# A hybrid decoder layer on one core: each attention pair projects its keys before its values, and the values of the last pair move into steps 44 to 48

## The chip, the cores and the metric

The kernel runs on one core of one Trainium2 chip. TensorE (PE) multiplies matrices, VectorE (DVE) and ScalarE (ACT) work on whole tiles and read the matmul results out of the PSUM banks, GpSimd (POOL) helps with plain elementwise work, and SyncE (SP) issues all the DMAs, in order, from one queue. Every engine works through its own list of instructions in the order in which the program wrote them, and waits on semaphores where an operand comes from another engine.

The metric is the time of one execution on the device in microseconds. Before the change it is 1214.67 us, the median of three runs (1214.23 to 1215.04).

## The reference

One decoder layer for 1024 tokens of width 1024, in fp32. The input is normalised and multiplied by one wide matrix; its columns feed two mixers, whose outputs are joined, normalised (the attention half), multiplied by the output matrix, normalised and added to the input. A squared-ReLU MLP of width 4096 follows in the same way.

```python
h = rmsnorm(x, mix_pre_norm)
q_a, k_a, v_a, q_h, f_h, i_h, g_h = split(h @ w_in)
attn = rmsnorm(dilated_mixture_attention(q_a, k_a, v_a, slopes), attn_out_norm)
rec  = hgrn2_recurrence(q_h, f_h, i_h, g_h, lower_bounds, hgrn_out_norm)
x = x + rmsnorm(concat([attn, rec]) @ w_out, mix_post_norm)
x = x + rmsnorm(square(relu(rmsnorm(x, mlp_pre_norm) @ w_ff1)) @ w_ff2, mlp_post_norm)
```

The attention has 8 heads of 64 columns. Each head mixes three causal windows, (window, dilation) = (128, 1), (512, 4) and (2048, 16), weighted by their softmax denominators. The recurrence has 4 heads of 128 columns with a gated state.

## The kernel before

**Precision.** The matmuls work on pairs of fp32r tiles: a value is split into a high part (ACT copies it) and a low part (DVE or POOL subtracts the high part from the value), and a product is three matmuls, high by high, low by high and high by low (`three_pass`, lines 89 to 91). So each weight block must be split before use: `w_split` copies on ACT (line 85) and subtracts on DVE (line 86), and then issues the load of a later raw block (line 106). `w_get(i, ahead)` splits all blocks of the weight stream up to number i + ahead. The blocks 16 to 27 are the query, value and key columns of the four pairs of heads; 28 to 35 are the eight row blocks of the output matrix (`WO0` is 28).

**Stages.** First come the four recurrence heads, then 64 attention steps, then the second part of the output product, the norms, and the MLP. The attention works in pairs of heads. For each pair, `attn_proj` (line 728) is a Python generator that emits the projections: queries, the values of the first 512 tokens, both halves of the keys, and the values of the other 512 tokens. One call emits one unit, which is three matmuls of 512 columns, and a 512-token half of a projection has eight units. After the eighth unit the PSUM bank is read: `keys_read` for the keys, line 747 for the queries (followed by two ACT copies and two POOL subtractions), line 764 for the values.

**The filler queue.** The generators stand in a list, `queue`, and `fill` (line 172) takes units from it. A generator that yields None stops the filling for that call. So the units are put between the attention work, step by step, as PE's filler: `UNITS` (line 1236) gives the number for each of the 64 steps, one half of them in the middle of the step and the others at its end. Two conditions stop the queue: the queries of pair 2 and 3 wait for `second_done`, the keys of a pair wait for `first_done` of the pair ahead, which is set in step 3 of its 16 steps, when those keys' slabs come free.

**The steps.** Each head has eight steps, one for each item: four blocks of local attention (D0 to D3), two far parts (F0, F1) and two near parts (N0, N1). A step takes the exponentials of the next item (`raise_`, ACT, line 892), multiplies queries by keys for a later item (`look`, PE; its maximum is taken on DVE, line 842), transposes the item's weights (`turn`, PE; copies on ACT and subtractions on DVE), multiplies the item before by the values (`weigh`), and finishes an earlier one (`finish`). The maximum of a far row is joined with that of the near rows between the items 0 and 4: `spread_max` (DVE, line 865) in items 0 and 2, `swap_max` (PE) in items 1 and 3, `joint` (DVE, lines 878 and 879) in items 3 and 4. The exponentials of the far part need `joint`. A PSUM bank with a look's result comes free when DVE has taken the maximum. At most one key job (half a pair's key split: ACT, POOL and two DMAs) runs per step.

**The values.** `values_turn` (line 712) transposes a half's values on PE, copies them on ACT (line 719) and subtracts on DVE (line 720). The transposed values of a pair are stored to DRAM (`v_dram`, line 723) and read back in another order by `far_load` (line 642), for the far parts. The first use is the product of F0, in step 5 of the pair's first head. `far_load` runs after the last turn for pair 0, in steps 15 and 31 for the pairs 1 and 2, and in the hook of step 48 for pair 3.

**Hooks.** `hooks` (line 1214) is an order written out by hand: what else a step does. Steps 0 and 2 multiply the gate of the last recurrence head. Steps 43 to 54 prepare the early output product: the recurrence half of the first 512 rows is loaded (`early_rows`, line 1007), scaled on POOL (`row_rec`), transposed and split (`row_turn`), and multiplied by the first four row blocks of the output matrix (`early_out`, 32 units), which then serve as filler up to step 63. `early_rows` and `early_sums` use buffers of the input's transposed blocks (`hT`), and so can only stand where the projections of the first token half, or of both, are done.

## Time and profile before

| what | us |
|---|---|
| median of three runs | 1214.67 |
| the profiled execution | 1214.51 |
| its span | 1212.7 |
| PE busy in the span | 1198.3 |
| DVE busy | 868.8 |
| ACT busy | 546.6 |
| POOL busy | 326.3 |

The recurrence ends and the attention steps start at about 306 us of the span; the steps end at about 520 us. The granted PE clock is full throughout. In a row of the timeline stand start, duration, engine, line, operation, output and inputs, shapes and count; a bracket at its end gives the idle time of the engine before it, and what ended it. In a row of the table by stretches stand the stretch, its length, the busy time of PE, of PE's weight loads, of DVE, ACT and POOL with their instruction counts, the PE clock, the DMA share and GB/s.

### The profile page before, as it was taken

Reading aid. Unit: us, or ns where it says so; the run is one execution under the profiler, and the core shown is the slowest. Engines: PE = TensorE matmul, PEld = TensorE weight load, DVE = VectorE, ACT = ScalarE, POOL = GpSimd, SP = SyncE. Lnnn points to the kernel's source line nnn. Section 1 sums busy time; section 2 is a strip of 40 time slices with the busy share of each in tenths; the row PEclk is TensorE's granted clock in tenths of the full one; section 3 lists DMA queues with packets and bytes.
Section 4 is the critical chain, followed back from the end, with each engine's and each line's share of the span. In section 5 each row is a group of like instructions: output and inputs, shape, how many; then the busy total and the mean of one; then the engine's idle time right before and its main releaser. Section 6 shows DMA issues by size and latency. Waiting matters only on the chain.

```text
span 1212.7 us, 17220 instructions
## 1 busy us (share of the span) xinstructions
PE 1198.3 (99%) x6350; PEld 1026.8 (85%) x6350; DVE 868.8 (72%) x1478; ACT 546.6 (45%) x1067; POOL 326.3 (27%) x321
## 2 busy tenths in 40 slices
PE   8999999999999999999999999999999999999998
PEld 8898989888888887888888888888888888888886
DVE  5697878777666767677689566766678554478796
ACT  7633333322565657755565222222234453534562
POOL 0110102022221213254230886575631000000022
PEclk9999999999999999999999999999999999999999
DMA  5231323123544546364514555553587534433337
GB/s 218 69 94 58 104 75 108 36 82 75 141 109 117 141 118 146 104 218 145 188 64 156 182 174 209 192 185 140 199 324 266 212 92 152 158 102 100 109 104 278
DMA packets 86483, 174.21 MB, mean 144 GB/s; under 512 B 12160, under 2 KB 38784, under 8 KB 86400
## 3 DMA queue, kind: packets, MB, share of 16 engines
q1 hardware_dynamic: 86400, 173.12, 44.0%
q8 instruction: 50, 0.82, 0.3%
q14 instruction: 33, 0.27, 0.1%
HBM read 117.76 MB, written 49.04 MB: 138 GB/s over the span
## 4 chain that ended last, share of the span: by engine, by line
PE 93%; DVE 2%; ACT 2%; DMA 1%; issue 1%; POOL 0%; SPq 0%; DVEq 0%; POOLq 0%; ACTq 0%
PE f L1940 18%; PE f2s L1940 7%; PE pig L91 2%; PE pig L89 2%; PE pig L90 2%; PE pl L480 2%; PE pwo L91 2%; PE pwo L89 2%; PE pwo L90 2%; PE pm_ak L89 1%; PE pm_f L89 1%; PE pm_ak L91 1%; PE pm_ak L90 1%; PE pm_f L91 1%; PE pm_f L90 1%; PE pm_av L89 1%
## 5 line engine op out<-in xcount | busy, mean ns | idle before, releaser
L86 DVE TENSOR_TENSOR al<-ar,ah 128x1024 fp32r<-128x1024 f32 x56 | 70.6, 1261 | 80.7 <-ACT ah L85 80.6
L1940 PE MATMUL f<-bh,ah 128*128 128x512 f32 x320 | 124.5, 389 | 0.0
L1940 PE MATMUL f<-bl,ah 128*128 128x512 f32 x320 | 124.5, 389 | 0.0
L1940 PE MATMUL f<-bh,al 128*128 128x512 f32 x320 | 124.5, 389 | 0.0
L85 ACT ACTIVATE ah<-ar 128x1024 fp32r<-128x1024 f32 x56 | 59.1, 1056 | 87.5 <-DMA ar<-actd 87.2
L1940 PEld LDWEIGHTS f<-bh,al 128*128 128x128 f32 x320 | 60.1, 188 | 12.6
L1940 PEld LDWEIGHTS f<-bl,ah 128*128 128x128 f32 x320 | 60.1, 188 | 12.5
L1940 PEld LDWEIGHTS f<-bh,ah 128*128 128x128 f32 x320 | 60.1, 188 | 12.3
L2014 POOL TENSOR_SCALAR lbl<-ssq 128x1 f32<-128x1 f32 x4 | 3.3, 819 | 245.7 <-ACT fd L2010 245.6
L1563 POOL TENSOR_TENSOR e<-x,e 128x512 f32<-128x512 f32 x14 | 21.6, 1540 | 131.0 <-DVE x L1514 123.8
L1940 PE MATMUL f2s<-bl,ah 128*128 128x512 f32 (+1 forms) x128 | 48.9, 382 | 0.0
L1940 PE MATMUL f2s<-bh,al 128*128 128x512 f32 (+1 forms) x128 | 48.9, 382 | 0.0
L1940 PE MATMUL f2s<-bh,ah 128*128 128x512 f32 (+1 forms) x128 | 48.9, 382 | 0.0
L671 POOL COPY tout<-traw 128x256 f32<-128x256 f32 x16 | 12.2, 763 | 107.9 <-DMA traw<-in_bias_tab_dram 74.2
L991 POOL TENSOR_TENSOR anat<-anat,stat 128x128 f32<-128x128 f32 (+1 forms) x24 | 13.4, 559 | 102.4 <-DVE anat L990 91.1
L86 DVE TENSOR_TENSOR bl<-br,bh 128x1024 fp32r<-128x1024 f32 x32 | 40.1, 1253 | 1.1 <-ACT bh L85 1.0
L1957 ACT ACTIVATE acc<-f 128x512 f32<-128x512 f32 x28 | 16.7, 598 | 49.4 <-PE f L1940 49.4
L86 DVE TENSOR_TENSOR wl<-raw,wh 128x1024 fp32r<-128x1024 f32 x23 | 30.1, 1310 | 10.9 <-ACT wh L85 10.9
L85 ACT ACTIVATE bh<-br 128x1024 fp32r<-128x1024 f32 x32 | 33.6, 1050 | 3.7 <-PE f L1940 2.4
L707 POOL TENSOR_TENSOR kl<-kf,kh 64x512 fp32r<-64x512 f32 x16 | 22.2, 1390 | 39.8 <-ACT kh L706 36.8
L751 POOL TENSOR_TENSOR ql<-qf,q 64x512 fp32r<-64x512 f32 x16 | 21.4, 1340 | 42.4 <-ACT q L750 41.8
L89 PE MATMUL pwo<-woh,mt 128*128 128x512 f32 x80 | 31.6, 395 | 0.0
(1702 smaller groups left out, 4022.5 us busy)
## 6 DMA issues: line engine op xcount, KB each, us to landing
ar<-actd SPq DMA_DIRECT2D x56, 512.0 KB, 3.7
br<-in_w_ff_dram SPq DMA_DIRECT2D x16, 1024.0 KB, 6.3
w1r<-in_w_ff_dram SPq DMA_DIRECT2D x14, 1024.0 KB, 6.5
raw<-in_w_in_dram SPq DMA_DIRECT2D x26, 512.0 KB, 4.0
actd<-e SPq DMA_DIRECT2D x17, 768.0 KB, 4.3
actd<-e SPq DMA_DIRECT2D x11, 1024.0 KB, 4.1
vd<-v SPq DMA_DIRECT2D x16, 256.0 KB, 3.9
raw<-in_w_out_dram SPq DMA_DIRECT2D x8, 512.0 KB, 3.7
```

Of the source, the lines that this page charges most:

```text
L85: S.activation(hi, src, AF.Copy)
L86: eng.tensor_tensor(out=lo, in0=src, in1=f32(hi), op=ALU.subtract)
L89: TE.matmul(dst, lhs[0], rhs[0], start=start, stop=False)
L90: TE.matmul(dst, lhs[0], rhs[1], start=False, stop=False)
L91: TE.matmul(dst, lhs[1], rhs[0], start=False, stop=stop)
L480: TE.matmul(pl[:, n % 2, :192], kt[:, n * P:(n + 1) * P], sets[u // 2][:, n % 4], start=True, stop=True)
L707: G.tensor_tensor(out=kl[a:b], in0=src, in1=f32(kh[a:b]), op=ALU.subtract)
L751: G.tensor_tensor(out=lo[a:b], in0=full[a:b], in1=f32(stacks[i]["q"][a:b, sl]), op=ALU.subtract)
L991: G.tensor_tensor(out=dst, in0=dst, in1=st["rd"][:, b].unsqueeze(2).to_broadcast([P, n, 64]), op=ALU.mult)
L1563: eng[0].tensor_tensor(out=e1[:, 3], in0=a21, in1=e1[:, 2], op=ALU.add)
L1940: TE.matmul(pm, a[:, j, c], b[:, j, d], start=start and j == 0 and q == 0, stop=stop and j == 1 and q == 2, skip_group_check=True)
L1957: S.activation(acc_at(p, i), pm, AF.Copy)
```

## The change

The change reorders the work of the attention stage; the matmuls, their operands and their number stay.

- The weight stream has the key columns ahead of the value columns in each pair, and `attn_proj` projects queries, both halves of the keys, then both halves of the values. All the keys of a pair, and with them all its values, now stand behind the condition on `first_done`.
- A half of the values is transposed during the second half's projection, the other half during the queries of the next pair. Each half is stored on its own: four stores of four blocks, and four stores of two blocks (the last two blocks are not needed). `far_load` reads all of the first tile, then the second, and is called in steps 18 and 34 for the pairs 1 and 2.
- For the last pair the values run in steps 44 to 48; the last turn and `far_load` stand in the hook of step 49, and the early output products start there. `early_rows` is called when the first half of these values is done.
- Output block 0 and 1 get slabs of their own, block 2 and 3 the shared weight buffers; they are split in the hooks of steps 42, 46, 48 and 50, the third with its subtraction on POOL. Before, it was 44, 45, 47 and 48.
- The last gate is multiplied in four pieces, in steps 0 to 3. A key job may run in all items but 0 and 5. `UNITS` has other numbers.

```diff
@@ the weight stream
-    for i in range(4 * HH, 4 * HH + 3 * (AH // 2)):
-        stream.append((w_in[i], None))
+    for i in range(4 * HH, 4 * HH + 3 * (AH // 2), 3):
+        for n in (0, 2, 1):
+            stream.append((w_in[i + n], None))
     WO0 = len(stream)
-    WO_TAG = (None, ("S", "S"), ("S", "BT"), None, ("S", "S"), ("S", "T"), ("T", "T"), ("T", "T"))
+    WO_TAG = (("S", "S"), ("S", "BT"), None, None, ("S", "S"), ("S", "T"), ("T", "T"), ("T", "T"))
@@ hgrn_core: gated(g4) in halves becomes gated(g2) in quarters
...
@@ far_load
-        for odd in range(2):
-            for c, p0, k0, n in ((0, 0, 64 * odd, P), (1, 0, P - P * odd, 64), (1, 64, P - P * odd, 64)):
...
+        for c in range(2):
+            for odd in range(2):
+                for c_, p0, k0, n in ((0, 0, 64 * odd, P), (1, 0, P - P * odd, 64), (1, 64, P - P * odd, 64)):
+                    if c_ == c:
...
@@ values_turn
-        if hf == 1:
-            for r in range(DIL):
-                nc.sync.dma_start(out=v_dram[pr][r].rearrange("(n i) c -> i n c", i=32),
-                                  in_=f32(vs[32 * r:32 * r + 32]).rearrange("p n h a d -> p n (h a d)"))
-            if pr == 0:
-                far_load(0)
+        b = slice(0, 4) if hf == 0 else slice(4, 6)
+        for r in range(DIL):
+            nc.sync.dma_start(out=v_dram[pr][r].rearrange("(n i) c -> i n c", i=32)[:, b],
+                              in_=f32(vs[32 * r:32 * r + 32, b]).rearrange("p n h a d -> p n (h a d)"))
+        turned_v[pr] += 1
+        if pr == 0 and hf == 1:
+            far_load(0)
@@ attn_proj, behind the queries
+        while pr > 0 and not first_done[pr - 1]:
+            yield None
+        wk = w_get(A0 + 3 * pr + 1, 0)
...
+        for hf in range(2):
+            for n, cost in enumerate(proj_t(wk, f"ak{pr}", hf, box)):
+                if n == 4 and hf == 0:
+                    w_get(A0 + 3 * pr + 1)
+                yield cost
+            keys_read(pr, box[0], hf)
+            yield 650.0
+        wv = w_get(A0 + 3 * pr + 2, 0)
+        for hf in range(2):
             for n, cost in enumerate(proj_t(wv, f"av{pr}", hf, box)):
-                if n == 4:
-                    w_get(A0 + 3 * pr + 1 + hf)
+                if n == 3 and hf == 1:
+                    values_turn()
+                    cost += 450.0
+                if n == 4 and hf == 0 and pr < AH // 2 - 1:
+                    w_get(A0 + 3 * pr + 2)
                 yield cost
...
-        yield from values(0)
-        while pr > 0 and not first_done[pr - 1]:
-            yield None
...
-        yield from values(1)
@@ hooks
         0: lambda: last_gate(0),
-        2: lambda: last_gate(1),
-        43: lambda: row_rec(0),
-        44: lambda: [row_rec(1), w_get(WO0, 0)],
-        45: lambda: w_get(WO0 + 1, 0),
-        46: lambda: row_turn(0, 0),
-        47: lambda: [drain(), w_get(WO0 + 2, 0), early_sums(), queue.extend(early_out(t) for t in range(NE))],
-        48: lambda: [values_turn("t"), far_load(AH // 2 - 1), w_get(WO0 + 3, 0), row_rec(2)],
-        49: lambda: [load_bias(AH - 1), row_rec(3)],
-        50: lambda: row_turn(1, 0),
-        52: lambda: [row_turn(2, 0), load_gain("gmix", "R", g_mix)],
-        54: lambda: row_turn(3, 0),
+        1: lambda: last_gate(1),
+        2: lambda: last_gate(2),
+        3: lambda: last_gate(3),
+        42: lambda: w_get(WO0, 0),
+        46: lambda: [w_get(WO0 + 1, 0), row_rec(0)],
+        47: lambda: [row_turn(0, 0), row_rec(1)],
+        48: lambda: [drain(), w_split(G)],
+        49: lambda: [values_turn("t"), far_load(AH // 2 - 1), early_sums(),
+                     queue.extend(early_out(t) for t in range(NE))],
+        50: lambda: [w_get(WO0 + 3, 0), row_rec(2), load_bias(AH - 1)],
+        51: lambda: row_rec(3),
+        52: lambda: [row_turn(1, 0), load_gain("gmix", "R", g_mix)],
+        54: lambda: row_turn(2, 0),
         55: lambda: [w_get(WO0 + 4, 0), row_load(0)],
-        57: lambda: [row_load(1), row_norm(0, (0,))],
-        58: lambda: row_norm(1, (0,)),
+        57: lambda: [row_load(1), row_turn(3, 0)],
+        58: lambda: [row_norm(t, (0,)) for t in range(2)],
...
-    UNITS = ((2, 3, 3, 4, 3, 3, 3, 3), (2, 3, 3, 4, 3, 3, 3, 3), (3, 3, 3, 4, 2, 3, 3, 2), (3, 3, 3, 4, 2, 3, 3, 2),
-             (3, 3, 3, 4, 2, 3, 3, 2), (3, 3, 3, 3, 2, 2, 1, 1), (2, 2, 2, 2, 1, 2, 2, 1), (2, 2, 2, 3, 2, 2, 2, 2))
+    UNITS = ((3, 3, 3, 3, 2, 3, 3, 2), (3, 3, 3, 3, 2, 3, 3, 2), (3, 3, 3, 3, 2, 3, 3, 2), (3, 3, 3, 3, 2, 3, 3, 2),
+             (3, 3, 3, 4, 2, 3, 3, 2), (3, 3, 3, 2, 4, 4, 3, 3), (2, 3, 2, 2, 2, 2, 2, 2), (2, 3, 2, 3, 2, 2, 2, 2))
@@ the step loop
-        if i in (1, 2, 3, 6, 7):
+        if i not in (0, 5):
             key_job()
-        if s in (15, 31):
-            far_load(s // 16 + 1)
+        if s in (18, 34):
+            while turned_v[s // 16] < 2:
+                fill(1.0)
+            far_load(s // 16)
```

More of the change, by code (lines that the diff above doesn't have):

```diff
@@ L606, in hgrn_core, with gated @@
         fill(1500 * scale)
[L608 to L610 removed]
+        def gated(g2):
+            for n in range(g2 * 2, g2 * 2 + 2):
+                V.scalar_tensor_tensor(gate[:, n], pos[n // 4][:, n % 4], rs[:, n:n + 1], gate[:, n],
                                        op0=ALU.mult, op1=ALU.mult)
[L612 removed]
+            if g2 == 3:
                 nc.sync.dma_start(out=mix_dram[:, h * P:(h + 1) * P].rearrange("(n p) d -> p n d", p=P), in_=gate)
@@ L616, in hgrn_core @@
             return gated
-        for g4 in range(2):
-            gated(g4)
+        for g2 in range(4):
+            gated(g2)
     halves = ((0, 64), (64, 128))
@@ L766, in values @@
             turn_later.append((pr, vs, full, hf))
-            yield 650.0
-        vs = slab("V8", f"v{pr}", F32R, (P, NT, 2, 2, 64))
-        yield from values(0)
-        while pr > 0 and not first_done[pr - 1]:
-            yield None
-        wk = w_get(A0 + 3 * pr + 2, 0)
-        for i in range(2):
-            stacks[i]["kh"] = slab("S", f"kh{pr}_{i}", F32R)
-            stacks[i]["kl"] = slab("S", f"kl{pr}_{i}", F32R)
-        pairs[pr] = (stacks, vs)
-        for hf in range(2):
-            for n, cost in enumerate(proj_t(wk, f"ak{pr}", hf, box)):
-                if n == 3 and hf == 0:
-                    values_turn()
-                    cost += 450.0
-                yield cost
-            keys_read(pr, box[0], hf)
             if hf == 0 and pr == AH // 2 - 1:
```

17 lines of the change are left out of this document (8 added, 9 removed).

## The prediction

> **What bounds the kernel now.** I read the busy shares on the page first, then busy time by ten-microsecond stretches of the attention stage, then the rows of single engines around the steps that the change touches.
>
> ```profile
> PE 1198.3 (99%) x6350; PEld 1026.8 (85%) x6350; DVE 868.8 (72%) x1478; ACT 546.6 (45%) x1067; POOL 326.3 (27%) x321
> ```
>
> ```profile
> core 0 of [0], span 1212.7 us
> ...
> 310.00:320.00 10.00, 9.42 (x55) 8.02 (x54) 7.33 (x28) 5.94 (x15) 2.99 (x3) 1.00 0.48 135
> 460.00:470.00 10.00, 8.97 (x61) 7.80 (x60) 8.38 (x17) 9.46 (x24) 7.17 (x5) 1.00 0.67 143
> 470.00:480.00 10.00, 8.72 (x58) 7.50 (x57) 9.27 (x34) 5.74 (x12) 1.86 (x2) 1.00 0.64 163
> 480.00:490.00 10.00, 8.80 (x58) 7.37 (x57) 5.37 (x16) 7.60 (x27) 0.80 (x2) 1.00 0.86 252
> ```
>
> PE is busy for 1198.3 of 1212.7 us, at full clock (the 1.00 of each stretch). The change removes no matmul and adds none, so the new time is the old one plus or minus PE's idle time. From 460 to 490 PE idles 1.03 + 1.28 + 1.20 = 3.5 us while DVE or ACT is nearly full: these are steps 45 to 53, where weight splits, the last value projection and the first early products meet. At 310 to 320 it idles 0.6 us (step 2). That is what there is to win. What can be lost is any place where PE gets less filler than the other engines need.
>
> **The change part by part.** Units first.
>
> ```profile
> 310.71 0.40 PE L89 MATMUL pm_aq<-hTh,wh 128*128 128x512 f32 x1
> ...
> 311.41 0.28 PE L873 MATMUL px<-pick,swap 128*128 128x4 f32 x2
> 312.27 0.36 PE L837 MATMUL ps_F<-kh,qc 128*128 128x192 f32 x1 [0.58 <-DVE stat L842]
> ```
>
> A projection unit (three matmuls) takes 311.41 - 310.71 = 0.70 us. I counted through the filler queue by hand which unit falls in which step, before and after.
>
> (a) The queue stops at step 2. Keys of pair 1 may not start before step 3 sets first_done[0]. Before, the values stood ahead of the keys and filled step 2. After, steps 0 and 1 use up the last six query units, and step 2 gets none of its three. Its cover is gone, and the last query unit now ends just ahead of it:
>
> ```profile
> 315.04 1.28 ACT L750 ACTIVATE q<-qf 64x512 fp32r<-64x512 f32 x2 [1.22 <-DVE qf L747]
> 316.35 0.39 ACT L951 ACTIVATE pf<-pov 128x256 f32<-128x256 f32 x1
> 316.76 0.46 ACT L892 ACTIVATE pf<-pf,stat 128x192 f32<-128x192 f32 x1
> 317.12 0.19 ACT L892 ACTIVATION_READ_ACCUMULATOR pf<-pf,stat 128x1 f32 x1
> 317.21 0.57 ACT L931 ACTIVATE pth<-pt_D 128x512 fp32r<-128x512 f32 x1
> 317.69 0.44 ACT L892 ACTIVATE pf<-pf,stat 128x192 f32<-128x192 f32 x1
> 318.04 0.19 ACT L892 ACTIVATION_READ_ACCUMULATOR pf<-pf,stat 128x1 f32 x1
> 318.13 1.04 ACT L85 ACTIVATE wh<-raw 128x1024 fp32r<-128x1024 f32 x1
> ```
>
> ```profile
> 314.32 0.68 DVE L747 SCALAR_TENSOR_TENSOR qf<-pm_aq,rrow 128x512 f32<-128x512 f32 x1
> 314.92 0.37 DVE L865 TENSOR_TENSOR swap<-stat,pick 128x128 f32<-128x128 f32 x1
> 315.14 1.11 DVE L610 SCALAR_TENSOR_TENSOR gate<-po,hrs,gate 128x128 f32<-128x128 f32 x4
> 316.16 0.15 DVE L878 TENSOR_TENSOR stat<-px,stat 128x4 f32<-128x4 f32 x1
> ```
>
> From the end of that unit, DVE reads the bank (0.68), ACT makes the two query copies (1.28), and only then the exponential of block D3, queued behind them (a 512-wide ACT pass lies between 0.57 and 1.04; I take 0.8 with its accumulator): with handovers 3.0 us. PE meanwhile has the swap, the F look, one turn and one small product, 1.3 us, so the turn of D3 waits 1.7. Next, the turn of F0 needs both halves of the F exponentials: a copy and a subtraction of D2 (about 1.0 together), swap 0.37, two gate pieces 0.55, joint (two passes like the 0.15 row, 0.3), then 0.65 + 0.57 + 0.65 on ACT, 4.1 us, against 2.9 us of PE work with three units: 1.2. Less the 0.58 that goes because half of the gate work has left step 0: +2.2 us (ends +0.5, if ACT catches up, and +3.5).
>
> (b) Weight splits that now stand ahead of the joint maximum. In every head the turn of F0 (item 4) waits for: spread, joint, exponential, copy, exponential. Before, no split stands between spread and joint. After, weight 22 is split at the end of step 10, 28 in the hook of step 42 and 31 in that of step 50, all in item 2.
>
> ```profile
> 450.74 0.34 PE L837 MATMUL ps_F<-kh,qc 128*128 128x192 f32 x1
> ...
> 457.01 0.62 PE L914 MATMUL pt_F<-ident,pf 128*128 128x128 f32 x3
> ```
>
> ```profile
> 452.84 0.39 DVE L865 TENSOR_TENSOR swap<-stat,pick 128x128 f32<-128x128 f32 x1
> ```
>
> ```profile
> L86 DVE TENSOR_TENSOR wl<-raw,wh 128x1024 fp32r<-128x1024 f32 x23 | 30.1, 1310 | 10.9 <-ACT wh L85 10.9
> ```
>
> Those are steps 42 to 44 of before: look at 450.74, spread done at 453.2, turn of F0 at 457.01 with six units between. With a split put in: ACT finishes its product copy at about 453.3, one key copy (0.64, half of the 1.28 row), the high part 1.04, then DVE the low part 1.31 (to 456.3), joint 0.3, and 0.65 + 0.57 + 0.65 on ACT: 458.4 to 458.5. Six units and the attention work (1.8) took 6.27, so a unit among other work is about 0.75. PE arrives with five units at 456.3 in step 44: +2.0. In step 12 six units lie between, arrival 457.0: +1.2. Ends 0 (the raw weight is early and ACT empty, a split of 1 us less) and +3.
>
> (c) Last-pair values in steps 44 to 48 and what hangs on them. In steps 44 to 47 PE gets 14 units instead of 6, and DVE loses three splits there, so the 3.5 us of idle time goes. But the early rows can only be loaded when the last product of the first token half is done, since they take its buffers: step 45 instead of 40, for a row turn in step 47.
>
> ```profile
> erows<-mixd SPq DMA_DIRECT2D x2, 512.0 KB, 6.2
> ```
>
> ```profile
> 467.27 1.30 POOL L1035 TENSOR_TENSOR erows<-erows,etable 128x512 f32<-128x512 f32 x1
> ```
>
> ```profile
> 462.39 0.22 PE L837 MATMUL ps_D<-kh,q 128*128 128x128 f32 x1
> ...
> 466.81 0.40 PE L89 MATMUL pwe<-wh,emt 128*128 128x512 f32 x1
> ```
>
> After that product: 0.5 to issue, 6.2 to land, 1.30 on POOL: 8.0 us. PE needs, up to the row turn, five units (3.7 with the changes of operand), the value turn (about 0.4), and the attention work of steps 46 and 47, which is 466.81 - 462.39 = 4.4 less one unit, one row turn and 0.85 of gaps, 2.4: together 6.5. Wait +1.5 (0 to 3; an earlier wait of DVE's would shrink it). Between the last value unit in step 48 and the first early product in step 49 PE has no unit at all: the F look waits for the N reductions behind the 1.1 us value read, +0.4 (0 to 1). Step 52 has the split of weight 31 with four units between, by the rows of (b) without the key copy: 7.05 us against 4.9: +2.0.
>
> (d) Far values. Pair 3's last turn moves to step 49, its first use stays in step 53; pair 2's moves from step 30 to 33, for step 37.
>
> ```profile
> 471.70 0.27 PE L716 MATMUL pvt<-ident,vf 128*128 128x128 f32 x1
> ...
> 487.95 0.30 PE L960 MATMUL pov_far<-ptFh,vf 128*128 128x128 f32 x1 [0.74 <-DMA vf<-vd]
> ```
>
> ```profile
> 473.69 3.04 SPq L723 DMA_DIRECT2D vd<-v  x4
> 479.44 3.64 SPq L642 DMA_DIRECT2D vf<-vd  x6
> ```
>
> Before, the way from turn to landed far block is 16.2 us: 2.0 to the first store issue, the issues 3.04, landing 2.7, six loads 3.64, and 4.9 to the last landing. Half stores may save 1 us. In the new step 49 the store waits longer: DVE has reductions and the last finish ahead of the subtraction, and SP has weight 32's load ahead, which waits for the POOL split: about 1.5 more, 16.7. PE's work between turn and use is 16.2 less the 0.74 of the row, less 1.74 of other idle time in the stretches 470 to 490, less the attention part of one item (half of the 2.4 in (c), 1.2) and one row turn (0.4): 12.1, and 14.1 with the wait in step 52. That leaves 2.6; the loads now come in the order of use, so I take +2.2 (0 to 5). Pair 2 has eleven units at 0.75 and three and a half items at 1.2, 12.4, against 15.2 by the row; but the DMA share was 0.86 there and is lower in steps 33 to 37, so I take +0.9 (0 to 3). Pair 1's loads start in step 18, eight units and three items ahead of their use in step 21, 9.6 us against 3.64 + 4.9: covered. The other stores, sixteen issues more in all, and the gate in four pieces instead of two (the same eight passes) lie beside PE work; so do the third and fourth row turn, one item later each, and the first squares of row 0, which move from step 57 to 58. In the recurrence before step 0 the second key half is read one level earlier and one level has three units instead of four: at most one unit, I take +0.4.
>
> (e) The split of weight 30 on POOL: 1.30 for 512 columns makes 2.6 us (an estimate from that row), for a use in step 51: covered. It can hold up DVE:
>
> ```profile
> 277.15 0.69 DVE L548 TENSOR_TENSOR kt<-kt,tot 128x512 f32<-128x512 f32 x1 [0.67 <-PE pl L544]
> 277.76 1.78 DVE L550 TENSOR_TENSOR qt<-qt,tot 128x512 f32<-128x512 f32 x1
> ```
>
> Two DVE passes of one size take 0.69 and 1.78 us; the second ran beside a key subtraction on POOL. So the split may cost DVE 1.1 us more in step 49, which lies in the 1.5 of (d). [...]
>
> **Sum.** 2.2 + (2.0 + 1.2) + (1.5 + 0.4 + 2.0 - 3.5) + (2.2 + 0.9 + 0.4) = +9.3 us. The profiled execution took 1214.5 us (span 1212.7 and 1.8 around it), 0.2 under the median of the runs. 1214.5 + 9.3 = 1223.8.
>
> **Rivals.** First, faster: the relief in steps 45 to 53 decides. Place: DVE's queue at 460 to 490; price: 3.5 us of idle time, and 0.6 at step 2. For it speaks that DVE is at 9.27 of 10 there and PE does wait for it. Against it, ACT and DVE still stand in a fixed order in front of each turn of F0. It decides if the new waits of (a) to (d) stay under 1.6 us in all: with 0.6 of them left, 1214.5 - 4.1 + 0.6 = 1211.0. Second, a draw: the split waits of (b) vanish because ACT and DVE run ahead of PE there, the loads land in time, and only (a) and the level remain, 2.6, against the relief with 0.9 still lost: 1214.5 + 2.6 - 2.6 = 1214.5. Third, the far blocks become the bound: the loads are slowed by 512 KB weight loads in the same queue, so that pairs 2 and 3 reach their upper ends, 5 + 3 instead of 3.1: 1228.7.
>
> **How the numbers follow.** Forecast (1217 to 1227) 0.62; far blocks late 0.18; draw 0.11; faster 0.08; slower still 0.01. The 10-us sum is many small waits of one kind, each from a queue order that I can read; its size is less sure than its sign. The range goes from 1214 (leaving out faster and half of the draw) to 1231. About 0.2% (2.4 us) is what a measurement can tell from no change. Slower 0.81, same 0.11, faster 0.08.
>
> **What would show it.** (a): PE idle at the turns of D3 and F0 in steps 3 and 4, released by ACT, 2 to 3 us between 312 and 320. (b): pt_F waiting for ACT in heads 1 and 5, over 1 us each. (c): the row turn waiting for POOL in step 47; the value, weight and row work no longer waited for at 464 to 477. (d): pov_far waiting for DMA in steps 37 and 53. Wrong if PE's idle time over the stage falls below 5 us, or if these rows are absent.

## The result

The changed kernel takes 1225.52 us (median of 6 runs, 1223.09 to 1227.84). The kernel before, in the 6 runs beside and before it, takes 1214.45 us (1213.78 to 1215.20). The ratio is 1.0092, with a 95% interval of 1.0079 to 1.0105: slower by 11 us. The forecast was 1223.8 us.

The profiled run of the changed kernel took 1223.09 us, 2.4 us less than its median (for the kernel before, the profiled run was 0.2 us from it). So 8.6 us of the loss can be read in this profile, and 2.4 us cannot. That second part turned out to be a matter of its own.

First the busy shares on the page of the changed kernel, and its row of the attention stage (stretch, length, busy time of PE, PEld, DVE, ACT and POOL, granted clock, DMA share, GB/s):

```profile
PE 1199.6 (98%) x6350; PEld 1027.6 (84%) x6350; DVE 862.6 (71%) x1477; ACT 547.0 (45%) x1067; POOL 325.4 (27%) x322
```

```profile
250.00:550.00 300.00, 287.39 (x1728) 249.10 (x1727) 199.21 (x547) 170.22 (x444) 81.19 (x99) 1.00 0.44 120
```

The span is 1221.3 us, against 1212.7 before. The same stretch of the kernel before:

```profile
250.00:550.00 300.00, 295.02 (x1772) 255.84 (x1771) 212.50 (x561) 174.71 (x458) 87.88 (x107) 1.00 0.47 129
```

PE does the same work (1198.3 us before, 1199.6 after), the clock is full, and PE's idle time from 250 to 550 goes from 300 - 295.02 = 5.0 to 300 - 287.39 = 12.6 us. That is 7.6 of the 8.6 us. What PE waited for, before and after (total, times, longest):

```profile
PE ps_F L837 <- DVE stat L842: 1.3, 2, 0.7
PE pt_N L911 <- DVE ptNl L932: 0.9, 2, 0.7
PE pov_far L960 <- DMA vf<-vd: 0.7, 1, 0.7
PE ps_N L837 <- DVE stat L842: 0.5, 1, 0.5
```

```profile
PE pt_F L916 <- ACT pf L894: 4.3, 7, 1.2
PE pmt L1080 <- POOL erows L1037: 2.7, 1, 2.7
PE pt_D L904 <- ACT pd L894: 1.6, 1, 1.6
PE pl L545 <- DVE tot L555: 1.2, 1, 1.2
PE pwe L89 <- ACT esum L1103: 1.0, 1, 1.0
PE pov_far L962 <- DMA vf<-vd: 0.8, 2, 0.5
PE ps_F L839 <- ACT wh L85: 0.5, 1, 0.5
```

DVE, which held PE up most before, is nearly gone from the list: the relief in steps 45 to 53 came as forecast. In its place stand ACT (the exponentials ahead of the turns of D3 and F0), POOL (the first early row) and one level of the recurrence. PE's rows say where (the bracket holds the idle time before the row and what ended it):

```profile
280.41 1.97 PE L545 MATMUL pl<-qt,kt 128*128 128x64 f32 x16 [1.21 <-DVE tot L555]
...
316.31 0.66 PE L904 MATMUL pt_D<-ident,pd 128*128 128x128 f32 x4 [1.62 <-ACT pd L894]
319.95 0.44 PE L916 MATMUL pt_F<-ident,pf 128*128 128x128 f32 x2 [0.41 <-ACT pf L894]
...
346.37 0.33 PE L916 MATMUL pt_F<-ident,pf 128*128 128x128 f32 x1 [0.25 <-ACT pf L894]
347.29 0.44 PE L916 MATMUL pt_F<-ident,pf 128*128 128x128 f32 x2 [0.59 <-ACT pf L894]
...
456.18 0.33 PE L916 MATMUL pt_F<-ident,pf 128*128 128x128 f32 x1 [1.23 <-ACT pf L894]
457.10 0.44 PE L916 MATMUL pt_F<-ident,pf 128*128 128x128 f32 x2 [0.59 <-ACT pf L894]
473.63 0.66 PE L1080 MATMUL pmt<-ident,erows 128*128 128x128 f32 x4 [2.72 <-POOL erows L1037]
...
479.64 0.33 PE L839 MATMUL ps_F<-kh,qc 128*128 128x192 f32 x1 [0.49 <-ACT wh L85]
488.24 0.33 PE L916 MATMUL pt_F<-ident,pf 128*128 128x128 f32 x1 [0.69 <-ACT pf L894]
489.16 0.44 PE L916 MATMUL pt_F<-ident,pf 128*128 128x128 f32 x2 [0.59 <-ACT pf L894]
...
494.63 0.30 PE L962 MATMUL pov_far<-ptFh,vf 128*128 128x128 f32 x1 [0.37 <-DMA vf<-vd]
```

From top to bottom: the recurrence level, steps 3 and 4, step 12, step 44, step 47, step 49, step 52 and the far block of step 53.

### The profile page after: what moved, and what is told of

It is laid out like the page before. It is cut to its first block, busy times and chain, and to the rows that moved or that the text cites. A ratio compares the mean times of both kernels' runs of the same rounds, so it can differ in the third digit from the quotient of the medians.

```text
span 1221.3 us, 17249 instructions
## 1 busy us (share of the span) xinstructions
PE 1199.6 (98%) x6350; PEld 1027.6 (84%) x6350; DVE 862.6 (71%) x1477; ACT 547.0 (45%) x1067; POOL 325.4 (27%) x322
## 4 chain that ended last, share of the span: by engine, by line
PE 92%; DVE 2%; ACT 2%; DMA 2%; issue 1%; SPq 1%; POOL 0%; DVEq 0%; POOLq 0%; ACTq 0%
PE f L1946 18%; PE f2s L1946 7%; PE pig L91 2%; PE pig L89 2%; PE pig L90 2%; PE pl L481 2%; PE pwo L91 2%; PE pwo L89 2%; PE pwo L90 2%; PE pm_f L89 1%; PE pm_f L91 1%; PE pm_f L90 1%; PE pm_aq L89 1%; PE pm_aq L91 1%; PE pm_aq L90 1%; PE pm_ak L89 1%
## 5 line engine op out<-in xcount | busy, mean ns | idle before, releaser
L1946 PEld LDWEIGHTS f<-bl,ah 128*128 128x128 f32 x320 | 60.1, 188 | 12.6
L674 POOL COPY tout<-traw 128x256 f32<-128x256 f32 x16 | 12.6, 786 | 110.2 <-DMA traw<-in_bias_tab_dram 79.8
L89 PE MATMUL pwo<-woh,mt 128*128 128x512 f32 x80 | 32.2, 402 | 0.0
L91 PE MATMUL pwo<-woh,mt 128*128 128x512 f32 x80 | 31.3, 391 | 0.0
L90 PE MATMUL pwo<-wol,mt 128*128 128x512 f32 x80 | 31.2, 391 | 0.0
```

What stands on the lines that cost most here:

```text
L89: TE.matmul(dst, lhs[0], rhs[0], start=start, stop=False)
L90: TE.matmul(dst, lhs[0], rhs[1], start=False, stop=False)
L91: TE.matmul(dst, lhs[1], rhs[0], start=False, stop=stop)
L674: G.tensor_copy(by_class(dst[:, part_ * w:(part_ + 1) * w]), in_blocks(raw[:, FAR * DIL:]))
L1946: TE.matmul(pm, a[:, j, c], b[:, j, d], start=start and j == 0 and q == 0, stop=stop and j == 1 and q == 2, skip_group_check=True)
```

## The experiments

The theory: the loss is a sum of separate waits of PE, each made by one place in the order of a queue. The rivals: (A) the waits are only a part, and a lower granted clock in the runs that were not profiled is the rest (these had a mean clock of 0.996 to 0.997, the profiled one 0.999); (B) DVE, ACT or the DMA queue is the true bound, so that a wait taken away comes back elsewhere. A further rival blames the added work itself: the POOL split and the sixteen added store issues.

All twelve results in one table. "Idle" is 300 us less PE's busy time from 250 to 550 in the kernel's profiled run; "half" is the time at a granted clock of 0.50 in the same stretch, in that profile.

| kernel | median us (lowest to highest, runs) | ratio to before, 95% | profiled run us | idle us | half us |
|---|---|---|---|---|---|
| before | 1214.45 (1213.78 to 1215.20, 6) | | 1214.51 | 5.0 | 0 |
| changed | 1225.52 (1223.09 to 1227.84, 6) | 1.0079 to 1.0105 | 1223.09 | 12.6 | 0 |
| row turn later | 1224.16 (1222.10 to 1226.01, 5) | 1.0069 to 1.0093 | 1222.10 | 10.6 | 3.4 |
| splits after joint | 1222.82 (1220.81 to 1227.26, 6) | 1.0063 to 1.0094 | 1227.26 | 12.7 | 10.2 |
| units for step 2 | 1223.82 (1222.11 to 1227.80, 5) | 1.0064 to 1.0090 | 1227.80 | 12.8 | 10.2 |
| row wait longer | 1230.70 (1229.82 to 1231.03, 4) | 1.0122 to 1.0148 | 1230.90 | 15.9 | 10.2 |
| three together | 1218.28 (1217.91 to 1219.24, 5) | 1.0020 to 1.0045 | 1219.24 | 8.1 | 3.4 |
| far loads first | 1218.15 (1215.64 to 1221.10, 8) | 1.0019 to 1.0039 | 1217.85 | 7.0 | 3.4 |
| level filled | 1216.62 (1214.38 to 1218.00, 11) | 1.0008 to 1.0026 | 1217.66 | 5.4 | 6.8 |
| before, step 2 empty | 1218.80 (1216.14 to 1220.67, 8) | 1.0025 to 1.0046 | 1217.32 | 7.5 | 0 |
| no POOL split | 1213.85 (1213.25 to 1215.74, 11) | 0.9988 to 1.0006 | 1213.34 | 4.2 | 0 |
| best order | 1213.80 (1212.84 to 1215.69, 11) | 0.9989 to 1.0006 | 1213.33 | 4.7 | 0 |
| stores in one | 1232.58 (1231.28 to 1233.73, 4) | 1.0136 to 1.0163 | 1231.49 | 17.2 | 10.2 |
| wait filled | 1226.30 (1225.81 to 1227.63, 4) | 1.0079 to 1.0113 | 1227.63 | 10.2 | 6.8 |

One sum fits these rows: the profiled time less the idle time and less half of the half-clock time is 1208.6 to 1210.5 us in every row but the last, where the 4.7 us of added products must be taken off as well (1209.3). So within about 1 us the whole case is idle time plus half-clock time. The runs of the changed kernel and of the first three edits spread over 4 to 6 us each, so their medians, which differ by 1.4 to 2.7 us, are not told apart by the times alone; there the rows of the profiles carry the argument.

### The first early row turn one step later

```diff
-        47: lambda: [row_turn(0, 0), row_rec(1)],
-        48: lambda: [drain(), w_split(G)],
+        47: lambda: row_rec(1),
+        48: lambda: [drain(), row_turn(0, 0), w_split(G)],
```

> The changed kernel with the first early row turn one step later (step 48 in place of 47). Theory (separate waits of PE, each with its own price): the row product is ready at about 473.6 and PE would reach the turn only after the last value unit, the turn of D0, the small products and the N look of step 48, some 3 us of work; the wait of 2.7 us falls to 0 to 0.5 us and the median goes from 1225.5 to about 1223.0. Rival A (the wait of about 3 us also lowers PE's granted clock in the runs that were not profiled, whose clock was 0.996 to 0.997 against 0.999): the clock is 0.999 in all runs and the median falls by some 2.4 us more, to 1220.6. Rival B (the wait only moves on, since DVE or SP is what PE waits for at the next place): within 1 us of 1225.5.

Measured: 1224.16 us, 1.4 less than the changed kernel. The 2.72 us wait is gone from the list of waits, and the idle time falls by 2.0 us; the far values take part of it back:

```profile
PE pov_far L962 <- DMA vf<-vd: 2.2, 4, 1.0
```

The far values went from 0.8 to 2.2 us. Only the part of the last pair lies behind the edit: its wait in step 53 goes from 0.37 to 1.01 us, since its transfers do not come earlier because PE does. The other 0.6 to 0.7 us are waits of pairs 1 and 2, ahead of step 47, and so differ from run to run. So the wait of step 47 was real, and about a quarter of it came back at the next transfer. The clock stayed at 0.995 to 0.997, so that one wait is not what lowers it: rival A as I wrote it here fell, though not the half clock itself, which the next runs show.

### The splits behind the joint maximum

```diff
-        42: lambda: w_get(WO0, 0),
+        43: lambda: w_get(WO0, 0),
...
-        50: lambda: [w_get(WO0 + 3, 0), row_rec(2), load_bias(AH - 1)],
-        51: lambda: row_rec(3),
+        50: lambda: [row_rec(2), load_bias(AH - 1)],
+        51: lambda: [w_get(WO0 + 3, 0), row_rec(3)],
...
-                if n == 4 and hf == 0 and pr < AH // 2 - 1:
+                if n == 6 and hf == 0 and pr < AH // 2 - 1:
```

> The changed kernel with the splits of weights 28 and 31 put one step later (hooks of steps 43 and 51), and that of each pair's next weight two units later, so that none stands between the spread of the maximum and the joint maximum. Theory: the waits of the turns of F0 in steps 12 (0.8 us), 44 (1.8) and 52 (1.3) go, 3.9 us; with 0.5 us given back at other places the median goes to about 1222. Rival B (these turns wait for the exponentials anyhow, with ACT as the bound): less than 1 us of 1225.5. Rival A (the clock): 0.996 to 0.997 as in the changed kernel.

Measured: 1222.82 us, 2.7 less. In the waits the turns of F0 fall from 4.3 to 0.4 us, all that was forecast for them:

```profile
PE pmt L1080 <- POOL erows L1037: 3.9, 1, 3.9
PE pov_far L962 <- DMA vf<-vd: 3.2, 3, 1.8
...
PE pt_F L916 <- ACT pf L894: 0.4, 1, 0.4
```

But the row turn's wait grew from 2.7 to 3.9 and the far values' from 0.8 to 3.2, since the rows and blocks land when they land. In this profiled run (the longest of its six) the idle time is not lower at all. The splits do make the waits of steps 12, 44 and 52; taking them away alone pays for a part of them only.

### Units for step 2

```diff
-    UNITS = ((3, 3, 3, 3, 2, 3, 3, 2), (3, 3, 3, 3, 2, 3, 3, 2), (3, 3, 3, 3, 2, 3, 3, 2), (3, 3, 3, 3, 2, 3, 3, 2),
+    UNITS = ((2, 2, 2, 3, 2, 3, 3, 2), (3, 3, 3, 3, 2, 3, 3, 2), (3, 3, 3, 3, 2, 3, 3, 2), (3, 3, 3, 3, 2, 3, 3, 2),
```

> The changed kernel with two units in each of steps 0, 1 and 2 of head 0 in place of three, three and none. Theory: the last query unit stays where it was seen from the queue, but PE has two units of 0.7 us in step 2, so the 2.0 us at the turns of D3 and F0 fall by about 1.4 us less what steps 0 and 1 lose by having one unit less (0 to 0.7): median about 1224.5. Rival (the last query read, wherever it stands ahead of the gate, holds ACT up by the same amount): no difference from 1225.5.

Measured: 1223.82 us, 1.7 less. The wait of 1.62 us for D3 is gone; one of 0.72 us for the F look at 314.75 stands in its place, and the far values wait 2.2 us. This profile, with its 10.2 us at half clock, shows what lowers the mean clock. Its rows by microsecond, behind the recurrence level's wait:

```profile
280.00:281.00 1.00, 0.16 (x2) 0.19 (x2) 1.00 (x3) 0.00 (x0) 0.15 (x1) 1.00 0.77 184
...
282.00:283.00 1.00, 1.00 (x10) 0.91 (x9) 0.15 (x1) 0.00 (x0) 0.00 (x0) 0.93 0.13 29
283.00:284.00 1.00, 1.00 (x4) 0.81 (x3) 1.00 (x2) 0.00 (x0) 0.00 (x0) 0.50 0.00 0
...
285.00:286.00 1.00, 1.00 (x4) 0.71 (x4) 0.96 (x1) 0.00 (x0) 0.00 (x0) 0.50 0.00 0
286.00:287.00 1.00, 1.00 (x5) 0.87 (x4) 0.00 (x0) 0.00 (x0) 0.00 (x0) 0.86 0.24 16
```

The granted clock (the third number from the end) is 0.50 from about 282.9 to 286.3, 3.4 us, and PE is busy throughout, with four matmuls to the microsecond. So the busy share shows nothing of it. In the changed kernel's own profile the same wait (1.21 us) is followed by a full clock.

### A longer wait, and the same wait filled

```diff
-        46: lambda: [w_get(WO0 + 1, 0), row_rec(0)],
+        46: lambda: [w_get(WO0 + 1, 0), row_idle(0), row_idle(0), row_rec(0)],
+    def row_idle(t):
+        G.tensor_tensor(out=early["table"][:, 0, :AW], in0=rec_row(t), in1=gains["early"], op=ALU.mult)
```

> The changed kernel with two more passes of 128x512 on POOL (into a buffer that is free there) ahead of the first row product, so that the wait of PE in step 47 grows by twice 1.30 us from 2.7 to about 5.3 us. Theory: the median goes up by 2.6 us to 1228.1, clock as in the changed kernel. Rival A (a wait of more than about 3 us lowers PE's granted clock): more than the 2.6 us, 1230 to 1232, with a granted clock of 0.996 or less also in the profiled run and a stretch with a clock under 1.00 behind the wait. Rival B (other waits behind it absorb it): less than 1 us.

Measured: 1230.70 us, 5.2 more, for 3.0 us of added wait: rival A's range. Then the same kernel with products in the wait:

```diff
         pt = bank("pv" if late else tag, f"pmt{t}_{which}")
+        if t == 0 and which == 0:
+            q = pairs[AH // 2 - 1][0][0]["q"]
+            for _ in range(20):
+                TE.matmul(pt, q[:, :P], q[:, :512], start=True, stop=True)
```

> The kernel with the longer wait (1230.7 us, 5.7 us of idle time ahead of the first early row turn and 6.8 us at half clock behind it), with twenty products of 128x512 that nobody reads put into that wait: each takes about 0.23 us of PE's time, 4.6 us in all, so PE is busy and the row turn waits for its last 1.1 us only. The turn itself comes at the same time as before, since POOL releases it. Theory (it is PE's idle time that draws the half clock, not the late release): the stretch at half clock behind step 47 is gone and the median falls by up to half of 6.8 us, to 1227.3 to 1228.5. Rival (the time behind the wait is lost to something else that waits on the late row, and the clock only shows it): 1230.7 within 0.7 us.

Measured: 1226.30 us, 4.4 less, with twenty matmuls more. PE's rows around the row turn, first with the wait empty, then with it filled:

```profile
478.27 1.11 PE L1083 MATMUL pmt<-ident,erows 128*128 128x128 f32 x4 [5.75 <-POOL erows L1037]
479.03 0.78 PE L89 MATMUL pm_av<-hTh,wh 128*128 128x512 f32 x1
479.61 0.63 PE L90 MATMUL pm_av<-hTl,wh 128*128 128x512 f32 x1
```

```profile
473.43 4.71 PE L1085 MATMUL pmt<-q 128*128 128x512 f32 x20
478.17 0.66 PE L1087 MATMUL pmt<-ident,erows 128*128 128x128 f32 x4
478.58 0.47 PE L89 MATMUL pm_av<-hTh,wh 128*128 128x512 f32 x1
478.89 0.39 PE L90 MATMUL pm_av<-hTl,wh 128*128 128x512 f32 x1
```

The turn itself comes at the same time, 478.27 and 478.17. Behind the empty wait the first two products stand 0.58 us apart and last 0.78 and 0.63 us, behind the filled one 0.31 us, and last 0.47 and 0.39. So in this pair of profiles it is PE's idle time that draws the half clock, not the late row. The gain is more than the forecast 2.2 to 3.4 us, and at most 3.4 of it (half of 6.8) can come from the stretch behind the filled wait. In the filled kernel two of the four runs have a mean clock of 1.000 (1225.8 and 1226.2 us), so there the half clock behind the other waits failed to come as well; the longer 1227.63 of its profiled run holds two half-clock stretches behind other waits, of 280 and of step 44.

### The three edits at once, and the far loads first

Three together are the edits of the first three experiments.

> The changed kernel with the first early row turn in step 48, the splits behind the joint maximum and two units in each of steps 0 to 2: the three edits of the first experiments at once. Theory (separate waits, but the far blocks' chain of the last pair does not move earlier when PE does): PE's idle time from 250 to 550 falls from 12.6 by 2.7 + 3.9 + 2.0 = 8.6 us to 4.0, and 2.5 to 4 us come back where the far values are waited for, so 6.5 to 8 us of idle time and one stretch at half clock (3.4 us long, 1.7 us lost) in an average run: median 1217 to 1220. Rival (the three only trade places, since DVE and ACT are the bound): 1222 or more.

Measured: 1218.28 us, within the forecast 1217 to 1220: 8.1 us of idle time, 3.2 of it for the far values. Rival B (1222 or more) fell, though a part of it holds: of the 8.6 us of waits that the edits remove, 4.1 come back at other places. Then the order of SP's queue in steps 48 and 49:

```diff
-        48: lambda: [drain(), row_turn(0, 0), w_split(G)],
-        49: lambda: [values_turn("t"), far_load(AH // 2 - 1), early_sums(),
+        48: lambda: [drain(), row_turn(0, 0)],
+        49: lambda: [values_turn("t"), far_load(AH // 2 - 1), w_split(G), early_sums(),
```

> As the three together, and the POOL split of weight 30 (with the weight load that waits for it in SP's queue) put behind the stores and loads of the last pair's far values, from step 48 to 49. Theory: SP's queue is free when the last value turn is stored, so the far blocks land about 2 us earlier (in the changed kernel the weight load was issued at 482.11 and the first store at 484.08) and the wait for them falls to 0 to 1.5 us: median 1214 to 1217. Rival B (the stores wait for the value read and its subtraction, not for SP): as the three together within 1 us.

Measured: 1218.15 us, no difference in the median, where 1214 to 1217 was expected. SP's rows, first of the three together, then with the far loads first:

```profile
476.05 0.36 SPq L106 DMA_DIRECT2D raw<-in_w_out_dram  x1
...
478.03 4.34 SPq L727 DMA_DIRECT2D vd<-v  x4
482.47 4.32 SPq L645 DMA_DIRECT2D vf<-vd  x6
```

```profile
477.04 2.97 SPq L727 DMA_DIRECT2D vd<-v  x4
480.12 4.28 SPq L645 DMA_DIRECT2D vf<-vd  x6
```

The loads leave 2.35 us earlier, as forecast, and the wait for the far values falls from 3.2 to 1.3 us; the last pair's is gone. But only 1.1 us of idle time goes (8.1 to 7.0): the POOL split now lies beside the spread of step 50 (1.69 us in its rows), and turns of F0 wait 1.2 us in place of 0.6. One wait went for another.

### The recurrence level

```diff
-                fill((3700 if li == 0 else 2900 if li < 3 else 2200) * scale)
+                fill((3700 if li == 0 else 2900 if li < 3 or li == 4 and scale > 1 else 2200) * scale)
...
-        fill(3000 * scale)
+        fill((2300 if scale > 1 else 3000) * scale)
```

> As the one with the far loads first, and the fifth level of the last recurrence head gets 2900 ns of filler in place of 2200, taken from the 3000 ns behind the levels. Theory: the wait of 1.2 us at 280 for DVE falls to 0 to 0.6 us, and with it goes the stretch at half clock that began 2 us behind it in two of five profiles: 0.6 to 1.5 us below the kernel with the far loads first. Rival (DVE's passes beside POOL's key subtraction set the time of the next level, whatever PE has to do): no difference.

Measured: 1216.62 us, 1.5 less. The two passes of DVE that made the wait, in the changed kernel:

```profile
277.13 1.45 DVE L549 TENSOR_TENSOR kt<-kt,tot 128x512 f32<-128x512 f32 x1 [1.13 <-PE pl L545]
278.50 1.76 DVE L551 TENSOR_TENSOR qt<-qt,tot 128x512 f32<-128x512 f32 x1
```

The wait at 280 is gone from the list, though these passes last as long as in the changed kernel (1.45 and 1.78 us beside POOL's key subtractions): PE has more to do meanwhile. The idle time is 5.4 us, as good as before the change, yet the median is 2.2 us over the kernel before, and the profile has 6.8 us at half clock behind 480.

### Without the POOL split, and one order more

```diff
-        47: lambda: row_rec(1),
+        47: lambda: [row_rec(1), w_split()],
...
-        49: lambda: [values_turn("t"), far_load(AH // 2 - 1), w_split(G), early_sums(),
+        49: lambda: [values_turn("t"), far_load(AH // 2 - 1), early_sums(),
```

> As the one with the level filled, with weight 30 split on DVE in step 47 in place of POOL in step 49. In the profile of the kernel with the level filled the spread of step 50 took 1.67 us beside the POOL split (0.37 to 0.39 alone). Theory (a POOL pass beside a DVE pass stretches the DVE pass, and so delays the joint maximum and the turn of F0 in step 52): the spread is back at 0.4 us, the waits at 479 to 483 (2.0 us in all) fall to 0.7 to 1.2, and with them the two stretches at half clock behind them become rarer: median 1214.5 to 1216 against 1216.6. Rival (the split is on no path, what waits there waits for weight 31): the waits at 479 to 483 stay at 2 us and the median within 0.5 us of 1216.6.

Measured: 1213.85 us, 2.8 less (1214.5 to 1216 was expected), and the same as the kernel before (0.9988 to 1.0006). DVE and POOL with the split on POOL:

```profile
475.10 2.39 POOL L86 TENSOR_TENSOR wl<-raw,wh 128x1024 fp32r<-128x1024 f32 x1
...
476.07 1.67 DVE L867 TENSOR_TENSOR swap<-stat,pick 128x128 f32<-128x128 f32 x1
...
477.45 1.33 POOL L1037 TENSOR_TENSOR erows<-erows,etable 128x512 f32<-128x512 f32 x1
...
477.79 1.01 DVE L881 TENSOR_SCALAR stat<-stat 128x4 f32<-128x4 f32 x1
```

and DVE without it:

```profile
475.55 0.56 DVE L867 TENSOR_TENSOR swap<-stat,pick 128x128 f32<-128x128 f32 x1
...
476.17 0.17 DVE L881 TENSOR_SCALAR stat<-stat 128x4 f32<-128x4 f32 x1
```

The spread of the maximum takes 0.56 in place of 1.67 us, and the 128x4 pass of the joint maximum 0.17 in place of 1.01. Beside one POOL pass after the other, small DVE passes on the path of the F0 turn lost 2 us. It ends two waits of the list and the half clock behind them.

Then weight 31 and the third and fourth row products moved as well:

```diff
-        if s in (18, 34):
+        if s in (17, 34):
...
-        49: lambda: [values_turn("t"), far_load(AH // 2 - 1), early_sums(),
+        49: lambda: [values_turn("t"), far_load(AH // 2 - 1), w_get(WO0 + 3, 0), early_sums(),
-        50: lambda: [row_rec(2), load_bias(AH - 1)],
-        51: lambda: [w_get(WO0 + 3, 0), row_rec(3)],
-        52: lambda: [row_turn(1, 0), load_gain("gmix", "R", g_mix)],
-        54: lambda: row_turn(2, 0),
+        50: lambda: load_bias(AH - 1),
+        52: lambda: [row_turn(1, 0), row_rec(2), load_gain("gmix", "R", g_mix)],
+        54: lambda: [row_turn(2, 0), row_rec(3)],
```

> As the one without the POOL split, and three more moves: weight 31 split in step 49 right behind the far loads, the third and fourth row products on POOL two and three steps later (52 and 54, away from the joint maxima of 51 and 52), and pair 1's far loads in step 17 in place of 18. Theory: the wait of 0.95 us at 375 for pair 1's far values goes, and the two waits for weight 31 (0.5 and 0.8) go, so PE's idle time from 250 to 550 falls from 5.4 to about 3 us (5.0 in the kernel before) and no wait over 1 us but the one for the early sum is left: median 1211.5 to 1213.5, below the kernel before at 1214.4. Rival (weight 31's split on DVE in step 49 holds up the reductions of F1 and moves the same wait to the turn of F0): 1214 to 1216.

Measured: 1213.80 us, no difference; the 1211.5 to 1213.5 that was expected was missed. The waits for weight 31 are gone, and the far values of pair 3 wait 1.36 us in their place. Neither version beats the kernel before by more than can be measured (1214.21 us in the 21 runs beside them).

### The queue stop in the kernel before

```diff
-    UNITS = ((2, 3, 3, 4, 3, 3, 3, 3), (2, 3, 3, 4, 3, 3, 3, 3), (3, 3, 3, 4, 2, 3, 3, 2), (3, 3, 3, 4, 2, 3, 3, 2),
+    UNITS = ((3, 3, 0, 4, 3, 3, 3, 3), (2, 3, 3, 4, 3, 3, 3, 3), (3, 3, 3, 4, 2, 3, 3, 2), (3, 3, 3, 4, 2, 3, 3, 2),
```

> The kernel before with three, three and no units in steps 0, 1 and 2 of head 0 in place of two, three and three: the values stand ahead of the keys as before, and only the cover of step 2 is gone (two units move to later steps). Theory: the turns of D3 and F0 wait as in the changed kernel, but no query read stands ahead of their exponentials, so 1 to 2 us of idle time: 1215.3 to 1216.3, without a lower clock. Rival (the cover of step 2 is not needed, and only the late query read made those waits): within 0.5 us of 1214.3. Rival A (such a wait also draws a stretch at half clock in part of the runs): up to 1.7 us more, 1217 to 1218.

Measured: 1218.80 us, 4.4 over the kernel before, above every range that was expected. The turn of D3 waits 1.55 us and that of F0 0.59, the same pair as in the changed kernel (1.62 and 0.41). The edit was less clean than I took it for: with three units in steps 0 and 1 the last query read does stand ahead of the gate here too, so it says nothing on that rival; and the two units that it lacks make the last keys late (1.70 us for the key block at 471). The idle time accounts for 2.5 of the 2.8 us by which its profiled run is over that of the kernel before. The median lies 1.5 us higher still, and the time of the eight runs goes with their mean clock: 1216.1 and 1217.1 us at 0.999, 1217.3 to 1218.9 at 0.998, 1219.3 to 1220.7 at 0.996 and 0.997. Behind which wait the clock fell is not shown, since the profile has no half clock in this stage.

### The value stores in one piece

```diff
-        b = slice(0, 4) if hf == 0 else slice(4, 6)
-        for r in range(DIL):
-            nc.sync.dma_start(out=v_dram[pr][r].rearrange("(n i) c -> i n c", i=32)[:, b],
-                              in_=f32(vs[32 * r:32 * r + 32, b]).rearrange("p n h a d -> p n (h a d)"))
+        for r in range(DIL if hf == 1 else 0):
+            nc.sync.dma_start(out=v_dram[pr][r].rearrange("(n i) c -> i n c", i=32)[:, :6],
+                              in_=f32(vs[32 * r:32 * r + 32, :6]).rearrange("p n h a d -> p n (h a d)"))
```

> The changed kernel with the value stores not halved: all six blocks of a lane are stored behind the second value turn, four issues a pair in place of eight. Theory: the first half's stores are on no path and the second half's issue takes as long for two blocks as for six, so the median stays at 1225.5 within 1 us and the wait for pair 3's far values at 0.4 to 1.4 us. Rival (the sixteen added DMA issues hold up SP's queue and make part of the loss): 1223 or less.

Measured: 1232.58 us, 7.1 over the changed kernel. Both the theory and the rival were wrong: the half stores, part of the change, are worth that much to it. SP's rows of pair 3, first with the half stores (the changed kernel), then without:

```profile
484.08 3.26 SPq L727 DMA_DIRECT2D vd<-v  x4
487.44 4.75 SPq L645 DMA_DIRECT2D vf<-vd  x6
```

```profile
487.56 4.17 SPq L726 DMA_DIRECT2D vd<-v  x4
493.86 3.49 SPq L645 DMA_DIRECT2D vf<-vd  x6
```

The stores of two blocks a lane are issued in 3.26 us, those of six in 4.17; and the first far load follows the last store after 0.1 us, where it stood back 2.1 us before. The wait for the far values rises from 0.8 to 5.3 us without the half stores, and the half-clock stretches with it.

## Why the prediction was right, and where it was not

The sign, the size and the mechanism held: many small waits in PE's queue, made by what stands ahead of what. Term by term, from the profiled run:

- (a) Queue stop at step 2: +2.2 forecast (the working gives 2.3). Measured 1.62 at the turn of D3 (1.7 forecast) and 0.41 at that of F0 (1.2 forecast), less the 0.58 of before: +1.4. The chain behind D3 was right; the one behind F0 ran beside the first wait and had less left to lose.
- (b) Splits ahead of the joint maximum: step 44 +2.0 forecast, 1.23 + 0.59 = 1.8 measured; step 12 +1.2 forecast (its own end of the chain, 458.4, less the arrival at 457.0 gives 1.4), 0.8 measured. Moving the splits took these waits away, so the cause is shown.
- (c) The relief came: the waits for DVE between 465 and 486 (2.6 us in the kernel before) are gone, and the rest of the 3.5 is the far wait that (d) counts too. The row turn of step 47 was forecast at +1.5 and took 2.72. PE reached it 6.4 us after the last product of the first half, as forecast (6.5). The rows took 9.1 us in place of 8.0: 0.6 to the issue, 7.2 from there to POOL's start where 6.2 was taken, and 1.3 on POOL. So the landing is what was mis-sized:

```profile
472.31 2.50 POOL L1037 TENSOR_TENSOR erows<-erows,etable 128x512 f32<-128x512 f32 x2 [7.04 <-DMA erows<-mixd]
```

  Step 49 +0.4, measured 0.5, but by luck: the profile names ACT's weight copy as what ended the wait, not DVE's reductions. Step 52 +2.0 (the working gives 2.2), measured 1.3.
- (d) Far values: pair 3 +2.2 forecast, 0.37 measured; pair 2 +0.9, measured 0; pair 1 "covered", measured 0.45. This is the term that failed: "Half stores may save 1 us". The rows above show 0.9 us on the issues and 2.0 us on the gap ahead of the loads, 2.9 in all; without the half stores pair 2 waits 1.6 us and pair 3 3.4. The recurrence level was forecast at +0.4 and measured at 1.21: the key subtractions on POOL now lie beside two DVE passes (1.45 and 1.76 us) with only three units to cover them.
- (e) The POOL split, called covered, and at most 1.1 us more on DVE inside another wait. In the changed kernel it does stand behind other waits: the two spreads nearest to it take 0.29 and 0.44 us, and the finish's small addition ahead of the value subtraction takes 0.62 us beside the split, where it took 0.16 in the kernel before; so 0.5 us were lost there. Once the other waits are gone the split costs: 2.8 us of the median from 1216.62 to 1213.85. The spread of step 50 took 1.67 us beside the split and 0.56 without it.

Of the signs that it named, two are missing or too small: no far wait stands in step 37, and the turn of F0 in head 1 waits 0.8 us where over 1 was named; the others are there. One wait is in no term, that for the early sum at the end of the steps (0.99 us, 0.50 before).

The errors cancel in part, so the sum of idle time is +7.6 where 9.3 was forecast. The other 3.5 of the median's +11.1 are in no term: 2.4 lie between the profiled run and the median and go, by an estimate from the mean clocks, with the half clock, and 1.0 in the profiled run is not traced to a place. That the forecast is only 1.7 us from the median is therefore partly luck: 1.7 us too much idle time, 3.5 us left out. The expectation was that PE stays "at full clock", read off the kernel before, whose longest wait from 250 to 550 us was 0.7 us. Of the rivals, the far blocks as the bound came nearest without the half stores (1.6 and 3.4 us for the pairs 2 and 3, where it named 3 and 5); the draw and the faster case did not come.

That the new order itself costs nothing is shown by the version without the POOL split: keys before values, with the same work, runs at 1213.85 against 1214.21 us. The loss was in where splits, the row turn and three units had been put around it. It gains nothing either: the relief at 460 to 490 is used up by waits for the early sum (1.0), weight 31 (0.8), the far values (0.8), the F look (0.7) and F0 (0.6).

## What to carry to other kernels

When work is moved in front of a fixed order, look for what now stands between a short reduction and the turn that waits for it: a split of 1 us on ACT and 1.3 us on DVE there cost PE 0.8 to 1.8 us. Waits that were taken away were paid back in part at other places (4.1 of the 8.6 us of the three edits), first of all at the next transfer, where the far values went from 0.8 to 3.2 us; so such edits are to be judged together. And a wait of PE could cost more than its length: one of 1.2 us was followed by 3.4 us at half clock in 3 of 9 profiles. Where a wait of 5.7 us was left in place, twenty products in it that nobody reads brought the median down by 4.4 us, up to 3.4 of them by the clock behind that wait.

## What the runs showed of the hardware that was not expected

The half clock came in pieces of one length. From 250 to 550 us the stretches in all profiles last 3.41 us, or twice that (6.83). Where one profile has two of them, their starts lie 191.1 us apart (282.9 and 474.0, units for step 2), 194.6 (282.6 and 477.2, row wait longer), 177.5 (281.7 and 459.2, wait filled) and 23.9 (471.6 and 495.5, splits after joint; 475.0 and 498.9, stores in one): about 56, 57, 52 and 7 times 3.41. What sets the starts is not shown.

The same wait drew a half clock in one profile and none in another. The wait of 1.21 or 1.22 us at 280, ahead of sixteen products of 64 columns, drew one in 3 of the 9 profiles that have it; the 1.8 us of step 44 in 1 of 6; the 1.6 us at D3 in none of 7; waits of 2.7 to 3.0 us in step 47 in 2 of 3, those of 3.9 and 5.7 us both times. In the three profiles that drew a half clock at 280, the 3.41 us ahead of it (from 278.3, 279.2 and 279.4) hold the whole wait and at least 1.6 us of the small products behind it. So a wait of 1.2 us was enough three times; why it was not in the other six profiles is not shown.

Each such stretch cost up to 1.7 us (half of 3.41), and about 1.4 of them in an average run would make the 2.4 us between the profiled run of the changed kernel and its median. Its other runs were not profiled, so this last step is an estimate; their mean clock (0.996 to 0.997 against 0.999) is what speaks for it, as 0.002 of 1225 us is 2.4 us, to about 1 us by the rounding of the clock.
